# FFN gate and up as seven block products with half of the output product between them

## The chip, the cores and the metric

One core of one Trainium2 chip runs the whole layer in one launch. The metric is the device time of that core in microseconds (us). Before the change three runs gave 1007.88, 1008.01 and 1008.09 us, a median of 1008.01 us.

The engines are called PE (matmul; PEld is its weight load), DVE (vector), ACT (scalar, activations and copies), POOL (GpSimd) and SP (the queue that issues most of the DMAs).

## The reference, cut to what matters

One layer: RMSNorm, a combined input projection, three token mixers, their merge, an output projection with a residual, then the feed-forward network (FFN) with a residual, then a final RMSNorm. The change touches the FFN only. There are 512 rows of 1024 channels; the hidden width is 2816, so 22 tiles of 128.

```python
h2 = rmsnorm(x, ffn_norm_g)
gate, up = jnp.split(h2 @ w_ffn_in, 2, axis=-1)      # (512, 1024) @ (1024, 2 * 2816)
return x + (jax.nn.silu(gate) * up) @ w_ffn_out      # (512, 2816) @ (2816, 1024)
```

## The kernel before

All numbers are float32. The kernel multiplies with three matmuls instead of one: each operand is split into a high part (a copy in fp32r, made by ACT) and a low part (the operand less its high part, made by DVE), and `mm3` (line 164) adds high x high, high x low and low x high into the same PSUM tile.

`h2` holds the normed activations transposed, channels on the partitions: eight tiles k of 128 channels by 512 rows, in two buffers of four k for the high parts and two for the low parts (class `HT`). `norm_B` (line 228) fills them, 128 rows at a time, from PSUM tiles into which PE has transposed the rows: for each half of the channels one copy on ACT and one subtraction on DVE.

The FFN runs over the 22 hidden tiles m (line 1130). For each m the weights of gate and of up (128 x 1024 each) are loaded by SP, split by ACT and DVE (`load_w`, line 159, and `parts`, line 149), and multiplied with h2: two PSUM tiles `ff`, 48 matmuls of 512 columns. ACT takes silu of the gate, DVE multiplies by up, ACT and DVE split the result into a high and a low part. These 22 pairs stay in SBUF, in `hid`, spread over buffers of several pools, because they are needed twice: after each odd m, `ffn_out` multiplies the last two of them with the left 512 output columns of the output weights, into four PSUM tiles `acc` that live through the loop (one for each 128 rows); after the loop all 22 are multiplied with the right 512 columns (`acc2`), in 18 steps over all rows and then the last four row by row, so that the final norm of the first rows runs beside the matmuls of the later ones. The tile m = 0 is done ahead of the loop, in two halves of 256 rows (`ff0`), so that its first half can start before the last 128 rows are normed.

PSUM has eight banks: three for `BIG` (pool pb), five for `SM` (pool pq). SBUF tiles come from pools with a fixed count of buffers for each tag: `w` (raw weights, 3), `wh` and `wl` (2 each), `u` (29 of 512 columns), `d` (8 of 1024), `t` (6 of 512), `o` (4 of 1024).

The order of each engine's queue is set by a scheduler at build time, from the order of the code, dependences, free buffers and priorities; at run time each engine works through its queue in that order. What stands in `tc.high_priority` is put ahead of what isn't, as soon as it has its buffers: the weights are prepared so, as far ahead as their buffers allow.

Of the kernel before, what the change touches and what calls it, by code (L numbers as in the profile page):

```python
# [16 lines left out]
P = 128  # L17
# [40 lines left out]
def trunk(ctx, tc, a, out, dbg=None):  # L58
# [105 lines left out]
    def mm3(ps, lh, ll, rh, rl, first, last):  # L164
        T.matmul(ps, lh, rh, start=first, stop=False)  # L165
        T.matmul(ps, lh, rl, start=False, stop=False)  # L166
        T.matmul(ps, ll, rh, start=False, stop=last)  # L167
# [60 lines left out]
    def norm_B(r, t, o):  # L228
        sl = slice(t * P, (t + 1) * P)
        for n, ph in enumerate(r):  # L230
            A.copy(o.h[n][:, :, sl], ph)
            V.tensor_tensor(o.l[n][:, :, sl], ph, o.h[n][:, :, sl].bitcast(F32), op=ALU.subtract)

# [58 lines left out]
    def cs(c):  # L292
        return slice(c * P, (c + 1) * P)
# [798 lines left out]

    def residual(t):
# [8 lines left out]
    ff0 = []  # L1102
    for t in range(NT):
# [3 lines left out]
        if t > 0:  # L1107
            norm_B(residual(t - 1), t - 1, h2)
    norm_B(residual(NT - 1), NT - 1, h2)
# [8 lines left out]

    acc = [SM("acc") for _ in range(NT)]
    fw = {}  # L1120
    hid = []

    def ffn_out(k, t, n, ps, c=slice(0, 512)):
        if (k // 2, n) not in fw:
            src = a["wfo"][2 * (k // 2):2 * (k // 2) + 2, :, 512 * n:512 * n + 512].rearrange("k p c -> p k c")
            fw[k // 2, n] = load_w(src)
        wh, wl = fw[k // 2, n]
# [4 lines left out]
    for m in range(FT):  # L1132
        pr = ff0 if m == 0 else []
        for g in range(2 if m else 0):
            wh, wl = load_w(a["wfi"][2 * m + g])
            ps = BIG("ff")
            for k in range(KT):
                mm3(ps, wh[:, cs(k)], wl[:, cs(k)], h2.hi(k), h2.lo(k), k == 0, k == KT - 1)
            pr.append(ps)
        s = TT("silu")  # L1140
        last = A.activation(s, pr[0], AF.Silu)
        V.tensor_tensor(s, s, pr[1], op=ALU.mult)  # L1142
        if m < 4:
            ho = op.tile([P, 2, S], F32R, tag="o", name=nm("ho"))
            hh, hl = ho[:, 0], ho[:, 1]
        elif m < 8:
            tg = ("toe", "pt", "sc", "kq")[m - 4]
            hh, hl = XT_("hh", tg, F32R), XT_("hl", tg, F32R)
        else:
            hh, hl = (DD if m < 8 + ND else UU)("hh", F32R)  # L1150
        A.copy(hh, s)
        V.tensor_tensor(hl, s, hh.bitcast(F32), op=ALU.subtract)
# [125 lines left out]
```

## Time and profile before

| | |
|---|---|
| median of three runs | 1008.01 us (1007.88 to 1008.09) |
| the profiled execution's own time | 1008.67 us |
| its span, first to last instruction | 1007.0 us |
| PE busy | 987.1 us, 98%, 5388 matmuls |
| DVE busy | 530.6 us, 53% |
| ACT busy | 442.9 us, 44% |
| POOL busy | 141.5 us, 14% |
| mean granted TensorE clock | 0.997 of full speed |
| moved by DMA | 98.31 MB, mean 98 GB/s |

The span is one execution, on the hardware profiler's clock. Busy times are sums over an engine's instructions; matmuls are pipelined and their records overlap, so the distance between the starts of two of them, not the length of a record, is what one costs in a stream. m = 0 of the FFN starts at 636.33 us, the loop with m = 1 at 649.14 us, and the final output leaves at the end of the span.

### The profile page before, as it was taken

The page shows a single profiled execution, that of the slowest core. Times are in us where ns is not written, and L with a number is a line of the kernel's source. Part 1 is how long each engine was busy: PE and PEld are TensorE (multiplying, and loading weights), DVE is VectorE, ACT ScalarE, POOL GpSimd, SP SyncE. Part 2 cuts the span into 40 slices and gives each one's busy share as a digit, 9 for nine tenths or more (in the row PEclk, how much of TensorE's full clock was granted, in tenths as well). Part 3 has the DMA queues.
Part 4 walks back from the last instruction along what each step waited for, and adds up shares of the span by engine and source line. Part 5 has one row for each costly group of instructions (what it writes and reads, how often), then busy time and mean ns, then how long its engine had stood idle before and what let it go on. Part 6 is the DMA issues. An engine that isn't in the chain of part 4 may idle for free.

```text
span 1007.0 us, 13645 instructions
## 1 busy us (share of the span) xinstructions
PE 987.1 (98%) x5388; PEld 810.6 (80%) x5388; DVE 530.6 (53%) x924; ACT 442.9 (44%) x715; POOL 141.5 (14%) x161
## 2 busy tenths in 40 slices
PE   6999999999999999999999999999999999999996
PEld 5788887778887778778888878988888888888885
DVE  6688846657755687665634355532332333323414
ACT  5376345544646476545535453422222222222313
POOL 5116020000223221341112120000000000000201
PEclk9999999999999999999999999999999999999999
DMA  6424261201222222122122224223222222222222
GB/s 217 169 84 126 87 207 63 75 32 55 102 87 82 84 67 81 58 90 84 64 105 84 105 105 168 84 85 104 102 86 105 88 100 105 85 104 99 90 104 84
DMA packets 33008, 98.31 MB, mean 98 GB/s; under 512 B 3504, under 2 KB 3776, under 8 KB 32944
## 3 DMA queue, kind: packets, MB, share of 16 engines
q1 hardware_dynamic: 31120, 91.14, 25.8%
q0 software_dynamic: 1824, 6.31, 2.3%
q8 instruction: 42, 0.69, 0.3%
q14 instruction: 22, 0.18, 0.1%
HBM read 91.65 MB, written 5.78 MB: 97 GB/s over the span
## 4 chain that ended last, share of the span: by engine, by line
PE 94%; DVE 3%; ACT 1%; DMA 1%; issue 1%; SPq 0%; POOL 0%; DVEq 0%; ACTq 0%; POOLq 0%
PE pj L165 10%; PE pj L166 10%; PE pj L167 10%; PE ff L167 8%; PE ff L165 8%; PE ff L166 8%; PE acc L166 4%; PE acc L165 4%; PE acc L167 4%; PE br L165 2%; PE br L167 2%; PE br L166 2%; PE ov L835 1%; PE pv L165 1%; PE pv L167 1%; PE pv L166 1%
## 5 line engine op out<-in xcount | busy, mean ns | idle before, releaser
L153 ACT CAST wh<-w 128x1024 fp32r<-128x1024 f32 x150 | 157.7, 1051 | 403.7 <-PE ff L166 163.9
L157 DVE TENSOR_TENSOR wl<-w,wh 128x1024 fp32r<-128x1024 f32 x148 | 194.0, 1311 | 251.4 <-ACT wh L153 248.6
L165 PE MATMUL pj<-hTh,wh 128*128 128x512 f32 x464 | 184.4, 397 | 1.0 <-DVE cvo L386 1.0
L166 PE MATMUL pj<-hTl,wh 128*128 128x512 f32 x464 | 183.4, 395 | 0.0
L167 PE MATMUL pj<-hTh,wl 128*128 128x512 f32 x464 | 182.7, 394 | 0.0
L165 PE MATMUL ff<-h2h,wh 128*128 128x512 f32 (+1 forms) x368 | 139.9, 380 | 0.0
L167 PE MATMUL ff<-h2h,wl 128*128 128x512 f32 (+1 forms) x368 | 139.8, 380 | 0.0
L166 PE MATMUL ff<-h2l,wh 128*128 128x512 f32 (+1 forms) x368 | 139.8, 380 | 0.0
L165 PEld LDWEIGHTS pj<-hTh,wh 128*128 128x128 f32 x464 | 87.2, 188 | 19.6 <-ACT wh L153 1.4
L167 PEld LDWEIGHTS pj<-hTh,wl 128*128 128x128 f32 x464 | 87.2, 188 | 17.3 <-issue 0.3
L166 PEld LDWEIGHTS pj<-hTl,wh 128*128 128x128 f32 x464 | 87.2, 188 | 16.5 <-issue 0.3
L166 PEld LDWEIGHTS ff<-h2l,wh 128*128 128x128 f32 x368 | 69.2, 188 | 13.2
L167 PEld LDWEIGHTS ff<-h2h,wl 128*128 128x128 f32 x368 | 69.2, 188 | 13.1
L165 PEld LDWEIGHTS ff<-h2h,wh 128*128 128x128 f32 x368 | 69.2, 188 | 13.0
L166 PE MATMUL acc<-wl,hh 128*128 128x512 f32 (+1 forms) x162 | 59.5, 367 | 0.0
L165 PE MATMUL acc<-wh,hh 128*128 128x512 f32 (+1 forms) x162 | 59.2, 366 | 0.0
L1182 POOL TENSOR_TENSOR x<-x,gb 128x512 f32<-128x512 f32 x4 | 6.0, 1539 | 343.6 <-ACT sq L197 343.6
L1142 DVE TENSOR_TENSOR silu<-silu,ff 128x512 f32<-128x512 f32 x22 | 15.1, 688 | 72.2 <-PE ff L167 72.2
L167 PE MATMUL acc<-wh,hh 128*128 128x512 f32 (+1 forms) x126 | 46.1, 366 | 0.0
L165 PE MATMUL br<-oh,wh 128*128 128x512 f32 x96 | 38.2, 398 | 0.0
L1042 POOL TENSOR_TENSOR y<-y,yt 128x512 f32<-128x512 f32 x16 | 22.5, 1406 | 110.6 <-DVE yt L1041 110.6
L167 PE MATMUL br<-oh,wl 128*128 128x512 f32 x96 | 37.7, 393 | 0.0
(320 smaller groups left out, 1590.3 us busy)
## 6 DMA issues: line engine op xcount, KB each, us to landing
w<-in_wb SPq DMA_DIRECT2D x60, 512.0 KB, 3.5
w<-in_wfi SPq DMA_DIRECT2D x44, 512.0 KB, 3.5
w<-in_wfo SPq DMA_DIRECT2D x22, 512.0 KB, 3.5
w<-in_wbr SPq DMA_DIRECT2D x12, 512.0 KB, 3.5
w<-in_wv SPq DMA_DIRECT2D x8, 512.0 KB, 3.4
w<-in_wout SPq DMA_DIRECT2D x8, 512.0 KB, 3.5
x<-in_x SPq DMA_DIRECT2D x4, 512.0 KB, 6.3
toe<-in_toe SPq DMA_DIRECT2D x8, 256.0 KB, 3.0
```

Of the source, the lines that this page charges most:

```text
L153: A.copy(hi, raw)
L157: (eng or V).tensor_tensor(lo, raw, hi.bitcast(F32), op=ALU.subtract)
L165: T.matmul(ps, lh, rh, start=first, stop=False)
L166: T.matmul(ps, lh, rl, start=False, stop=False)
L167: T.matmul(ps, ll, rh, start=False, stop=last)
L835: T.matmul(po[64 * hh:64 * hh + 64, 0:P], av[kt][:, h * 64:(h + 1) * 64], PT[hh][:, cs(kt)], start=kt == 0, stop=kt == qb, tile_position=( ...
L1042: G.tensor_tensor(y[m], y[m], t, op=ALU.add)
L1142: V.tensor_tensor(s, s, pr[1], op=ALU.mult)
L1182: G.tensor_tensor(xt[0], xt[0], gb[:, 0:512], op=ALU.mult)
```

## The change

For each m from 1 to 21 gate and up are computed together as one block product. The weights of the pair are seen as 2 x 2 blocks (gate or up, by first or second half of the 1024 channels), h2 as 2 x 2 blocks (half of the channels, by half of the rows). Seven products of blocks, with sums and differences of blocks as their operands, replace the eight of the direct way. A product is 4 k-tiles x 3 matmuls of 256 columns.

- The four sums of h2's blocks (T1 to T4) are made once, ahead of the loop, from unsplit copies `xf` that `norm_B` now leaves beside the split ones, and are then split; T4 overwrites a quarter of h2. The three sums of the weights' blocks (`s2`, `s3` and `s2` again) are made for each m by DVE and POOL and split by ACT and DVE, in `ffn_weights`, at high priority.
- Seven products go into three PSUM tiles `pa`, `pm`, `pg` (the three BIG banks), which are each used twice or three times in one m; between, ACT and DVE read them and add up gate and up (`c1`, `u2`, `u3`) in 256-column pieces. A later product accumulates on an earlier one in the same bank.
- Between the third and the fourth product stands `out_half(m - 1)`: the left half of the output product for the hidden tile before, with its own output weights loaded by SP and split, one k at a time.
- Each hidden tile is stored to DRAM (`hd`) by a DMA that ACT issues, and split into two buffers for `out_half`. For the right half of the output product each is loaded back (`hr`) and split a second time.

The diff, with the part that only deletes the old loop shortened:

```diff
--- before.py
+++ after.py
@@ -161,10 +161,11 @@
         with tc.high_priority(offset=HP):
             return parts(load_raw(src, n), n)
 
-    def mm3(ps, lh, ll, rh, rl, first, last):
-        T.matmul(ps, lh, rh, start=first, stop=False)
-        T.matmul(ps, lh, rl, start=False, stop=False)
-        T.matmul(ps, ll, rh, start=False, stop=last)
+    def mm3(ps, lh, ll, rh, rl, first, last, goes_on=False):
+
+        T.matmul(ps, lh, rh, start=first, stop=False, skip_group_check=goes_on)
+        T.matmul(ps, lh, rl, start=False, stop=False, skip_group_check=goes_on)
+        T.matmul(ps, ll, rh, start=False, stop=last, skip_group_check=goes_on)
 
     def preload(after):
 
@@ -225,11 +226,12 @@
             r.append(h4(ps))
         return r
 
-    def norm_B(r, t, o):
+    def norm_B(r, t, o, xf):
         sl = slice(t * P, (t + 1) * P)
         for n, ph in enumerate(r):
             A.copy(o.h[n][:, :, sl], ph)
             V.tensor_tensor(o.l[n][:, :, sl], ph, o.h[n][:, :, sl].bitcast(F32), op=ALU.subtract)
+            A.copy(xf[n][t // 2][:, :, (t % 2) * P:(t % 2) * P + P], ph)
 
     class HT:
 
@@ -1090,6 +1092,8 @@
     h2 = HT("h2")
     w0 = [load_w(a["wfi"][g]) for g in range(2)]
 
+    xf = [[op.tile([P, 4, 256], F32, tag="o", name=nm("xf")) for _ in range(2)] for _ in range(2)]
+
     def residual(t):
         xt = [U("x2") for _ in range(2)]
         for n in range(2):
@@ -1099,14 +1103,13 @@
         x2.append(xt)
         return norm_A(xt, rms_factor(xt), halves(gb), BIG if t < 2 else SM)
 
-    ff0 = []
     for t in range(NT):
         for n in range(2):
             for k in range(KB, KT):
                 out_mm(k, t, n, wo[k, n])
         if t > 0:
-            norm_B(residual(t - 1), t - 1, h2)
-    norm_B(residual(NT - 1), NT - 1, h2)
+            norm_B(residual(t - 1), t - 1, h2, xf)
+    norm_B(residual(NT - 1), NT - 1, h2, xf)
     ff0 = [BIG("ff") for _ in range(2)]
     for half in range(2):
         r = slice(256 * half, 256 * half + 256)
@@ -1116,45 +1119,139 @@
     tap("x2", x2[0][0])
 
 
+
+
+    LH, RH = slice(0, 256), slice(256, 512)
     acc = [SM("acc") for _ in range(NT)]
-    fw = {}
-    hid = []
+    hd = dr.tile([FT * P, S], F32, name="hd")
+
+    def split(src, hi, lo):
+        A.copy(hi, src)
+        V.tensor_tensor(lo, src, hi.bitcast(F32), op=ALU.subtract)
+        return hi, lo
+
+    def hidden(m, h):
+
+        A.dma_start(hd[m * P:(m + 1) * P, :], h)
+        return split(h, *DD("hh", F32R))
+
+    def out_half(k, hp_):
+        with tc.high_priority(offset=HP):
+            raw = XT_("wo", "toe")
+            nc.sync.dma_start(raw, a["wfo"][k, :, 0:512])
+            wh, wl = split(raw, XT_("woh", "pt", F32R), XT_("wol", "sc", F32R))
+        for t in range(NT):
+            mm3(acc[t], hp_[0][:, cs(t)], hp_[1][:, cs(t)], wh, wl, k == 0, k == FT - 1)
+
+    s0, h0 = TT("silu"), U("hid")
+    A.activation(s0, ff0[0], AF.Silu)
+    V.tensor_tensor(h0, s0, ff0[1], op=ALU.mult)
+
+    with tc.high_priority(offset=HP):
+        (x11, x12), (x21, x22) = xf
+        V.tensor_tensor(x11, x12, x11, op=ALU.subtract)
+        G.tensor_tensor(x12, x22, x12, op=ALU.subtract)
+        V.tensor_tensor(x22, x22, x11, op=ALU.subtract)
+
+        def tparts(src, s):
+            return split(src, *[dp.tile([P, 4, 256], F32R, tag="d", name=nm(s + c)) for c in "hl"])
+
+        T2 = tparts(x22, "T2")
+        V.tensor_tensor(x21, x21, x22, op=ALU.subtract)
+        T3 = tparts(x12, "T3")
+        T1 = tparts(x11, "T1")
+
+        T4 = split(x21, h2.h[0][:, :, RH], h2.l[0][:, :, RH])
+    hparts = hidden(0, h0)
+    B11, B21, B22 = [(h2.h[j][:, :, r], h2.l[j][:, :, r]) for j, r in ((0, LH), (1, LH), (1, RH))]
+
+    def cols(p, r):
+        return p[0][:, r], p[1][:, r]
+
+    def ffn_weights(m):
+        with tc.high_priority(offset=HP):
+            L_, R_ = slice(0, 512), slice(512, 1024)
+            u = load_raw(a["wfi"][2 * m + 1])
+            if m % 2:
+                g = load_raw(a["wfi"][2 * m])
+                a11, a12 = halves(g)
+            else:
+                a11, a12 = U("a11"), U("a12")
+                for n, d in enumerate((a11, a12)):
+                    nc.sync.dma_start(d, a["wfi"][2 * m, :, 512 * n:512 * n + 512])
+            a21, a22 = halves(u)
+            s3, s2 = U("s3"), U("s2")
+            gp = [wp.tile([P, 1024], F32R, tag=c, name=nm(c), bufs=2) for c in ("wh", "wl")]
+            up_ = [op.tile([P, 1024], F32R, tag="o", name=nm("wu")) for _ in range(2)]
+            if m % 2:
+                split(g, *gp)
+            else:
+                split(a11, *cols(gp, L_))
+            G.tensor_tensor(s3, a11, a21, op=ALU.subtract)
+            V.tensor_tensor(s2, a22, s3, op=ALU.subtract)
+            r = {1: cols(gp, L_), 2: cols(gp, R_), 5: cols(up_, L_), 4: cols(up_, R_)}
+            r[6] = split(s2, *UU("s2p", F32R))
+            r[7] = split(s3, *UU("s3p", F32R))
+            G.tensor_tensor(a21, a21, a22, op=ALU.add)
+            if not m % 2:
+                split(a12, *cols(gp, R_))
+            V.tensor_tensor(s2, a12, s2, op=ALU.subtract)
+            split(u, *up_)
+            r[3] = split(s2, *UU("s4p", F32R))
+        return r
+
+    def ffn_pair(m, hp_):
+        w = ffn_weights(m)
+        pa, pm, pg = [BIG("ff")[:, LH] for _ in range(3)]
+        e1, e2, h = TT("e1"), TT("e2"), U("hid")
+        c1, u2, u3, g1 = e1[:, LH], e1[:, RH], e2[:, LH], e2[:, RH]
+
+        def product(i, ps, b, first):
+            for k in range(4):
+                mm3(ps, w[i][0][:, cs(k)], w[i][1][:, cs(k)], b[0][:, k], b[1][:, k], first and k == 0, k == 3,
+                    not first)
+
+        product(1, pa, B11, True)
+        A.copy(c1, pa)
+        product(6, pm, T2, True)
+        V.tensor_tensor(u2, pm, c1, op=ALU.add)
+        product(7, pg, T3, True)
+        V.tensor_tensor(u3, pg, c1, op=ALU.add)
+        out_half(m - 1, hp_)
+        product(2, pa, B21, False)
+        A.activation(g1, pa, AF.Silu)
+        product(5, pm, T1, False)
+        V.tensor_tensor(u3, pm, u3, op=ALU.add)
+        product(4, pg, T4, False)
+        V.tensor_tensor(u2, pg, u2, op=ALU.add)
+        V.tensor_tensor(h[:, LH], g1, u2, op=ALU.mult)
+        product(3, pm, B22, False)
+        V.tensor_tensor(c1, pm, c1, op=ALU.add)
+        last = A.activation(c1, c1, AF.Silu)
+        V.tensor_tensor(h[:, RH], c1, u3, op=ALU.mult)
+        return last, hidden(m, h)
+
+    for m in range(1, FT):
+        last, hparts = ffn_pair(m, hparts)
+    out_half(FT - 1, hparts)
+
+
+    fw, hid = {}, {}
 
     def ffn_out(k, t, n, ps, c=slice(0, 512)):
-        if (k // 2, n) not in fw:
-            src = a["wfo"][2 * (k // 2):2 * (k // 2) + 2, :, 512 * n:512 * n + 512].rearrange("k p c -> p k c")
-            fw[k // 2, n] = load_w(src)
-        wh, wl = fw[k // 2, n]
+        if k not in hid:
+            if k % 2 == 0:
+                src = a["wfo"][k:k + 2, :, 512 * n:512 * n + 512].rearrange("k p c -> p k c")
+                fw[k // 2] = load_w(src)
+            with tc.high_priority(offset=HP):
+                raw = U("hr")
+                nc.sync.dma_start(raw, hd[k * P:(k + 1) * P, :])
+                hid[k] = split(raw, *DD("hh", F32R))
+        wh, wl = fw[k // 2]
         hh, hl = hid[k]
         r = slice(512 * (k % 2) + c.start, 512 * (k % 2) + c.stop)
         mm3(ps[:, c], hh[:, cs(t)], hl[:, cs(t)], wh[:, r], wl[:, r], k == 0, k == FT - 1)
 
-    for m in range(FT):
...
-            for k in (m - 1, m):
-                for t in range(NT):
-                    ffn_out(k, t, 0, acc[t])
     preload(last)
     gb = bc_row(2)
 ```

## Rows read from the trace of the kernel before

**Rows 1.** The page, part 1: busy us, share of the span, instructions.
```profile
PE 987.1 (98%) x5388; PEld 810.6 (80%) x5388; DVE 530.6 (53%) x924; ACT 442.9 (44%) x715; POOL 141.5 (14%) x161
```

**Rows 2.** The page, part 4: shares of the chain that ended last.
```profile
PE 94%; DVE 3%; ACT 1%; DMA 1%; issue 1%; SPq 0%; POOL 0%; DVEq 0%; ACTq 0%; POOLq 0%
```

**Rows 3.** Windows, FFN loop: length, busy PE, PEld, DVE, ACT, POOL; clock, DMA, GB/s.
```profile
649.40:932.10 282.70, 282.70 (x1249) 234.07 (x1248) 90.78 (x94) 78.51 (x96) 0.00 (x0) 1.00 0.28 99
```

**Rows 4.** Timeline, PE: first and last of one m's 48 (start, length).
```profile
703.57 0.39 PE L165 MATMUL ff<-h2h,wh 128*128 128x512 f32 x1
...
714.23 0.39 PE L167 MATMUL ff<-h2h,wl 128*128 128x512 f32 x1
```

**Rows 5.** Timeline, PE: the 256-column stream of m = 0, 65 matmuls; next m's first.
```profile
641.35 0.28 PE L166 MATMUL ff<-h2l,wh 128*128 128x256 f32 x1
...
649.02 0.28 PE L167 MATMUL ff<-h2h,wl 128*128 128x256 f32 x1
649.14 0.40 PE L165 MATMUL ff<-h2h,wh 128*128 128x512 f32 x1
```

**Rows 6.** Timeline, DVE and ACT after the last product of that m.
```profile
714.72 0.69 DVE L1142 TENSOR_TENSOR silu<-silu,ff 128x512 f32<-128x512 f32 x1 [3.38 <-PE ff L167]
715.51 1.23 DVE L157 TENSOR_TENSOR wl<-w,wh 128x1024 fp32r<-128x1024 f32 x1
716.66 0.68 DVE L1152 TENSOR_TENSOR hl<-silu,hh 128x512 fp32r<-128x512 f32 x1
...
714.42 1.05 ACT L153 CAST wh<-w 128x1024 fp32r<-128x1024 f32 x1 [3.85 <-PE ff L166]
715.44 0.62 ACT L1151 CAST hh<-silu 128x512 fp32r<-128x512 f32 x1
```

**Rows 7.** Timeline, DVE and POOL at the merge's end.
```profile
551.28 0.68 DVE L1063 TENSOR_TENSOR yh<-y,yh 128x512 fp32r<-128x512 f32 x1
551.88 2.31 DVE L157 TENSOR_TENSOR wl<-w,wh 128x1024 fp32r<-128x1024 f32 x1
...
548.73 1.29 POOL L1042 TENSOR_TENSOR y<-y,yt 128x512 f32<-128x512 f32 x1 [12.38 <-DVE yt L1041]
551.45 1.67 POOL L1042 TENSOR_TENSOR y<-y,yt 128x512 f32<-128x512 f32 x1 [1.43 <-DVE yt L1041]
```

**Rows 8.** Timeline, DVE and POOL in the mixers.
```profile
300.78 0.68 DVE L785 TENSOR_TENSOR kl<-pj,k 64x512 fp32r<-64x512 f32 x1
304.64 0.42 DVE L907 TENSOR_TENSOR kq<-kq,lqk 128x256 f32<-128x256 f32 x1
304.98 0.42 DVE L908 TENSOR_TENSOR kq<-kq,lqk 128x256 f32<-128x256 f32 x1
...
299.87 1.46 POOL L904 TENSOR_TENSOR kq<-g 128x256 f32<-128x256 f32 x1 [10.44 <-PE lv L885]
```

**Rows 9.** Groups by line and shape, ACT: busy us, mean ns; idle before.
```profile
L828 ACT COPY PT<-pT 128x256 f32<-128x256 f32 x8 | 2.9, 372 | 1.9 <-PE pT L826 1.9
L197 ACT ACTIVATE sq<-x 128x256 f32<-128x256 f32 x2 | 0.8, 416 | 1.0 <-DVE x L1177 1.0
```

**Rows 10.** The page, part 6 (KB, us to landing); then timeline, SP: one issue.
```profile
w<-in_wfi SPq DMA_DIRECT2D x44, 512.0 KB, 3.5
...
640.71 0.38 SPq L118 DMA_DIRECT2D w<-in_wfo  x1
```

**Rows 11.** Timeline, ACT and DVE in the norm's end; groups, POOL, 1024-wide.
```profile
636.17 1.08 ACT L231 CAST h2h<-nT 128x512 fp32r<-128x512 f32 x2 [0.47 <-PE nT L224]
637.13 0.65 ACT L197 ACTIVATE sq<-x 128x512 f32<-128x512 f32 x1
640.77 1.25 ACT L231 CAST h2h<-nT 128x512 fp32r<-128x512 f32 x2 [2.00 <-PE nT L224]
...
641.39 1.35 DVE L232 TENSOR_TENSOR h2l<-nT,h2h 128x512 fp32r<-128x512 f32 x2 [0.70 <-ACT h2h L231]
...
L157 POOL TENSOR_TENSOR wl<-w,wh 128x1024 fp32r<-128x1024 f32 x2 | 4.8, 2398 | 4.5 <-ACT wh L153 4.5
```

More of the change, by code (lines that the diff above doesn't have):

```diff
@@ L1130, in ffn_out @@
         mm3(ps[:, c], hh[:, cs(t)], hl[:, cs(t)], wh[:, r], wl[:, r], k == 0, k == FT - 1)
-    for m in range(FT):
[L1133 to L1152, printed above, removed]
-        hid.append((hh, hl))
-        if m % 2 == 1:
-            for k in (m - 1, m):
-                for t in range(NT):
-                    ffn_out(k, t, 0, acc[t])
     preload(last)
```

## The prediction, before the changed kernel was run

> **What bounds the kernel now.** I read the busy times first: PE is busy 987.1 of 1007.0 us, DVE 530.6, ACT 442.9, POOL 141.5 [rows 1]. A busy PE alone could be a waiting one, so next the chain that ended last: 94% of it is PE, 3% DVE [rows 2]. Then the stage that the change rewrites, cut out by time: from 649.40 to 932.10 us PE is busy 282.70 of 282.70 us at granted clock 1.00, DVE 90.78 (32%), ACT 78.51 (28%), POOL nothing [rows 3]. So nothing there waits but the helpers; the stage lasts as long as its matmuls, and its only price is the spacing of matmul starts. (A record's own length, 0.39 us, overlaps the next and prices nothing.) That spacing is 10.66 us over 47 steps, 0.2268 us for 512 columns [rows 4]. DVE and ACT have two thirds of their time free, and this is what the change spends.
>
> The profiled execution took 1008.67 us, its span 1007.0, so 1.67 us lie around it; the median of the runs is 1008.01. I make the sum as differences and set it on 1008.0.
>
> **The products.** For each m from 1 to 21 gate and up were 2 x 8 x 3 = 48 matmuls of 512 columns: 48 x 0.2268 = 10.89 us. They become 7 x 4 x 3 = 84 of 256 columns (12.5% fewer columns, 75% more instructions). The trace has such a stream, m = 0, which runs in halves of 256: 7.67 us for 64 steps, 0.1198 us [rows 5], not half of 0.2268 (0.1134). So 84 x 0.1198 = 10.06 us, 0.83 less for each m, and 21 x 0.83 = 17.4 us at most. The point at which nothing is gained is 10.89 / 84 = 0.1296 us a step. The output half, 12 matmuls of 512 for each m, stays: 2.72 us. The period of one m goes from 13.61 to 12.78 us.
>
> The Trainium skill (TensorE: Matmul & The Clock Gate, Back-to-back issue gap) gives an isolated gap of N/2.4 + 2.5 ns, 215.8 and 109.2 ns here, and warns that weight loads shape a real stream. By it each m would save 1.19 us and the whole 24.9. The stream of 256 shows 119.8 ns, so the row decides, and this extra gain gets 2 chances in 100.
>
> **DVE in the loop.** Each m now has: two 1024-wide subtractions (low parts of gate and up), seven of 512 (s2 twice, s2p, s3p, s4p, the output weights' low part, the hidden tile's), and seven of 256 (u2 twice, u3 twice, c1, two multiplications). Back to back, starts lie 1.15 us apart for 1024 [rows 6], 0.60 for 512 [rows 7] and 0.34 for 256 [rows 8]: 2.30 + 4.20 + 2.38 = 8.9 us. Each alone takes 1.23, 0.68 and 0.42: 10.2 us. Even m split gate in two of 512, 0.05 more. POOL gets two 512-wide operations, 1.29 us alone; the 1024 subtraction that met one took 2.31 us instead of 1.23, so each costs DVE up to 1.08 [rows 7]. Sum 11.1 to 12.4 us of 12.78: 87 to 97%. DVE isn't the bound, but no longer idle.
>
> The same rows hold for which operations? `kl`, which reads PSUM and one SBUF tile, took 0.68 us beside a POOL operation begun 0.91 us earlier [rows 8], no more than 512-wide ones with POOL idle. The Trainium skill (SBUF — State Buffer, Who interferes with whom) says that a DVE instruction with at most one SBUF input doesn't contend with GpSimd. The adds that free PSUM here have one SBUF input; by the rule they're only queued behind held ones. If they were held themselves, each tight one below would lose 0.3 us.
>
> **ACT in the loop:** 2 x 1.05 (1024-wide), five copies of 0.62 [rows 6], one of 0.37 from PSUM and two silus of about 0.42 at 256 columns [rows 9], and the store of the hidden tile, now issued from ACT: at 0 to 0.38 us, which the SP record shows for one issue [rows 10]. 6.4 to 6.8 us of 12.78; hidden.
>
> **The new waits in the loop.** The three PSUM banks are written two or three times in one m, so PE now waits for readers. Five of seven products have 4 us or more between reader and next writer. Two don't: product 3 writes pm when u3 has read product 5, with product 4 between; the next m's product 6 writes pm when c1 has read product 3, with product 1 between. Count from the start of the last matmul: record 0.28, hop to DVE 0.10 (714.62 to 714.72 [rows 4, 6]), the add 0.42, a hop back of about 0.06 (DVE to ACT took 0.03, 715.41 to 715.44): 0.86. PE is there after 13 x 0.12 = 1.56. So 0.70 us may go by in DVE's queue. Behind the add in that queue stand the other epilogue operations and the next weights; ahead of it can stand weights of m + 2, which have the higher priority. A 512 subtraction (0.60) is covered; a 1024 one just begun (1.15) costs 0.45; one held by POOL (2.31 - 0.08) costs 1.5. Bounds per m: 0 and 2 x 1.5 = 3.0. Rows 6 show the case: the low part of the hidden tile stood behind a 1024 one. A given add meets a 1024 one in 2 x 1.15 / 12.78 = 18% of phases and loses little (0.45² / 2 / 1.15 = 0.09); a held one in about as many and loses 0.5. That is near 0.1 an add, 0.2 an m: 4.2 us. I take it.
>
> The hidden tile: product 3, c1, silu, multiplication, store issue, copy, subtraction: 0.38 + 0.42 + 0.45 + 0.45 + 0.38 + 0.65 + 0.71 = 3.4 us; the output half's third matmul, the first to read the low part, is 13 matmuls of 0.12 per product times three later, 0.12 + 4.31 + 0.45 = 4.9. Cover 1.5 us; cost 0, at the most 3 x 1.15 - 1.5 = 2.0 an m if all three DVE steps meet a 1024 one.
>
> The weights come a whole m ahead (two buffers of each), and 512 KB land in 3.5 us [rows 10]; SP has the output weights, the split even gates and, later, the reloads in its one queue, with a period to spare: 0. If that cover went, a late weight would cost up to 3.5 us once.
>
> **Before the loop.** norm_B gets two more copies for each t, 0.55 us each on ACT. Those of t = 2 stand ahead of the square at 637.13, those of t = 3 beside the casts at 640.77 [rows 11]. That chain ends with h2l at 642.74 and slips by 1.1 + 0.55 to 644.4. The second half of m = 0 began 48 x 0.1198 = 5.75 us before 649.14, at 643.4: 1.0 us late (bounds 0 and 1.65). Then the sums and differences: x11 1.15, x12 on POOL 2.4 (its 1024-wide operations [rows 11]), x22 1.15, T2's parts 1.05 and 1.23: 7.0 us from 644.4, 651.4; with one weight subtraction between 652.6. Product 6 is there at 644.4 + 5.75 + 1.44 = 651.6. I take 0.5 (0 to 4.6, three further subtractions and a POOL hold ahead). Together 1.5.
>
> **After it.** Between the last product and the last output half lie 3.4 us, with nothing of the loop to fill them; the second half's matmuls can be put there if their reloaded tiles are in. I take 1.0 (0 to 3.4). The second half: each k has 2.72 us of PE and gains 0.62 on ACT and 0.68 on DVE beside half a weight tile (0.53 and 0.61): hidden, 0. DMA gets 22 stores and 22 loads of 256 KB, 11.5 MB, on queues that are busy 0.28 of that stage [rows 3]: 0.
>
> **Sum:** -17.4 + 4.2 + 1.5 + 1.0 = -10.7 us; 1008.0 - 10.7 = 997.3.
>
> **Rivals.** *A, the adds stand behind the weights (slower).* Place: u3 and c1 on DVE, in each m. For it: DVE 87 to 97% full, weights first, POOL holds. Against it: a 512 subtraction, the commonest, is covered. If both meet a fresh 1024 one: 0.9 x 21 = 18.9; 1008.0 - 17.4 + 2.5 + 18.9 = 1012. It turns the gain when the mean stall passes (17.4 - 2.5) / 21 = 0.71 us an m. Chance 0.20.
> *B, the hidden tile comes late.* One held subtraction (2.23) in its chain less the cover 1.5: 0.73 x 21 = 15.3; 1008.4, no change. For it: three DVE and three ACT steps in turn. Against: that they are spread over three products. Chance 0.12.
> *C, nothing is late.* DVE's operations fall between the adds, the ends are filled: 1008.0 - 17.4 + 1 = 991.6. For it: 1.5 us cover and free ACT. Against: two windows of 0.70. Chance 0.13.
> The forecast has 0.53, the wider spacing gain 0.02.
>
> **Range and chances.** The forecast's own range is 993 to 1004. C brings the low end to 991, A the high one to 1012; beyond lie A with POOL holds and the extra spacing gain, 2 in 10 or less. A change under 0.2% (2 us) can't be told from none here. Forecast, C and the extra gain are faster, 0.68, and of A and B 0.04; slower is most of A and a third of B, 0.19; the rest, 0.09, is within.
>
> **What would show it.** Right: starts of 0.120 us through the products; a period of one m near 13.0 us; PE's idle time ahead of product 3 and of product 6, released by DVE's u3 and c1; DVE near 75 to 90% of the loop and some 512 or 1024 subtractions at more than their 0.68 and 1.23; PE idle 1 to 2 us near 650 and 1 us at the loop's end. B would show as idle time ahead of the output half, released by the hidden tile's parts. Wrong: a spacing of 0.13 or more in the products, PE waiting for weights or a DMA, or a period over 13.6 us.

## The result, and the profile after

The changed kernel took 1083.17 us (median of 4 runs, 1080.68 to 1086.01) beside 1008.03 of the kernel before: ratio 1.0747, 95% interval 1.072 to 1.0773. The forecast was 997.3 with a range of 991 to 1012, so sign and size were wrong. The profiled execution took 1083.01 us, its span 1081.2.

The page of the changed kernel, parts 1, 2 (the 40 slices of PE and of its granted clock) and 4, against [rows 1, 2]:

```profile
PE 1004.8 (93%) x6144; PEld 858.5 (79%) x6144; DVE 694.0 (64%) x1205; ACT 511.4 (47%) x875; POOL 207.4 (19%) x204
...
PE   6999999999999999999999996988889888899896
...
PEclk9999999999999999999999998888999889999999
...
PE 86%; DVE 6%; ACT 3%; issue 2%; DMA 2%; POOL 0%; ACTq 0%; SPq 0%; DVEq 0%; POOLq 0%
```

PE is no longer the whole chain (94% before, 86% now), and both its busy share and its clock have fallen in one place, from slice 25 on (648.7 us): the rewritten stage. Its windows (length; busy PE, PEld, DVE, ACT, POOL with counts; clock, DMA share, GB/s), where [rows 3] had PE busy without a gap at clock 1.00:

```profile
649.60:673.30 23.70, 16.33 (x95) 14.70 (x94) 17.29 (x21) 8.38 (x12) 3.18 (x2) 0.78 0.26 89
673.30:1003.40 330.10, 285.06 (x1920) 268.09 (x1920) 220.29 (x332) 121.75 (x211) 57.69 (x39) 0.91 0.29 94
1003.40:1010.75 7.35, 4.46 (x14) 3.50 (x14) 4.29 (x8) 5.41 (x8) 0.00 (x0) 0.77 0.98 341
```

These are the first m, the other twenty, and the last output product. Each m has one add of c1 behind its product 3 (line 1229), so the instructions of that line (duration min/median/max in ns, start of the first and the last) measure the period:

```profile
L1229 DVE TENSOR_TENSOR e<-ff,e x21: 411/419/425, 673.5 to 1003.5; 128x256 f32<-128x256 f32 x21
```

(1003.5 - 673.5) / 20 = 16.50 us for one m; 13.61 before, 12.98 forecast. Against the forecast:

| part of the span | forecast, us | after, us |
|---|---|---|
| to the first add of c1 | 649.1 + 1.5 + 12.8 = 663.4 | 673.5 |
| twenty m's | 20 x 12.98 = 259.6 | 330.0 |
| from the last add of c1 to the end | 1.0 + 2.7 + 69.5 = 73.2 | 77.7 |
| span | 996.2 | 1081.2 |

(69.5 us lie in the trace of before between the end of its 22nd output half, 937.5, and 1007.0.) Of the 85 us missed, 70 lie in the steady m's, 10 in the first and 4.5 at the end.

**One pair of m's.** The stalls come at every second m. Windows of the changed kernel, one pair of 33.6 us:

```profile
864.00:871.90 7.90, 7.90 (x57) 7.35 (x55) 2.91 (x7) 1.01 (x2) 0.00 (x0) 1.00 0.50 170
871.90:877.30 5.40, 0.69 (x5) 0.35 (x3) 4.74 (x5) 3.25 (x6) 4.84 (x4) 0.93 0.15 53
877.30:884.00 6.70, 6.70 (x31) 6.51 (x32) 6.67 (x8) 2.75 (x5) 1.04 (x1) 0.54 0.20 56
884.00:897.60 13.60, 13.37 (x103) 12.76 (x102) 7.78 (x16) 5.02 (x9) 0.00 (x0) 1.00 0.20 68
```

PE stops for some 5 us, and then works at clock 0.54. Its timeline there (start, length, and in brackets the idle time before and its releaser):

```profile
871.76 0.28 PE L168 MATMUL ff<-h2h,s4p 128*128 128x256 f32 x1
874.97 0.38 PE L166 MATMUL ff<-h2h,wh 128*128 128x256 f32 x1 [2.93 <-ACT wh L1129]
875.20 0.28 PE L167 MATMUL ff<-h2l,wh 128*128 128x256 f32 x1
877.25 0.58 PE L168 MATMUL ff<-h2h,wl 128*128 128x256 f32 x1 [1.77 <-DVE wl L1130]
877.63 0.41 PE L166 MATMUL ff<-h2h,wh 128*128 128x256 f32 x1
...
881.90 0.41 PE L168 MATMUL ff<-T2h,s2p 128*128 128x256 f32 x1
```

Product 1 of the even m waits for the high part of its own gate weights, and two matmuls later for the low part: some 5.2 us beyond the normal spacing (874.97 - 871.88 and 877.25 - 875.32, plus one slow step). The 20 steps from 877.63 to 881.90 are 0.2135 us each, not 0.12: 1.9 us lost, 2.7 with the other slow matmuls. 2 x 12.78 + 5.2 + 2.7 = 33.5. The chain of waits through that place (start, length, what):

```profile
872.08 0.44 DVE e L1229
872.54 0.43 ACT e L1230
872.99 0.87 DVE hid L1231
873.88 0.33 ACTq L1135
874.30 1.15 ACT wh L1129 x2
875.45 1.75 DVE wl L1130
```

It runs from the last add of an odd m over the hidden tile (silu, multiplication, store) into the weights of the *next* m, which should have been ready long before, and on to PE at 877.25. The other engines in that place:

```profile
868.47 0.33 SPq L1141 DMA_DIRECT2D wo<-in_wfo  x1
868.85 0.90 SPq L1181 DMA_DIRECT2D a<-in_wfi  x2
...
872.30 1.26 POOL L1190 TENSOR_TENSOR s<-a,w 128x512 f32<-128x512 f32 x1 [27.96 <-DMA a<-in_wfi]
...
872.99 0.86 DVE L1231 TENSOR_TENSOR hid<-e,e 128x256 f32<-128x256 f32 x1 [0.48 <-ACT e L1230]
873.77 1.75 DVE L1191 TENSOR_TENSOR s<-w,s 128x512 f32<-128x512 f32 x1
875.44 3.44 DVE L1130 TENSOR_TENSOR wl<-a,wh 128x512 fp32r<-128x512 f32 x2
```

SP issues the gate halves of the even m only at 868.85, behind an output weight; POOL had stood 27.96 us for them; and DVE begins with s2 directly behind the hidden tile's last multiplication. With POOL now at work beside them, two low parts take 3.44 us and s2 1.75, where a 512-wide one alone takes 0.68 [rows 7]. The waits of the twenty m's (us in total, times, longest):

```profile
POOL s L1190 <- DMA a<-in_wfi: 161.3, 6, 28.2
POOL s L1190 <- DVE hid L1227: 80.8, 3, 27.5
...
PE ff L166 <- ACT wh L1129: 25.8, 10, 2.9
...
PE ff L168 <- DVE wl L1130: 16.6, 10, 1.9
```

The second row is the odd one: POOL's s3, a sum of weights, is put down to line 1227, the first write of the *hidden tile* of the m ahead. Nothing in the arithmetic ties these two together. What they share is the tag of their buffers: `hid`, `a11`, `a12`, `s3`, `s2` and the split sums all come from `U(...)`. That gave theory A: buffers of one tag are given out in the order of the code, so the tiles of m + 1, which stand behind `h` of m in the code, can't be begun before `h` is, near the end of m.

The row that gave the theory can't carry it, though. At m = 2 the same s3 runs ahead of that write:

```profile
671.98 1.29 POOL L1190 TENSOR_TENSOR s<-a,w 128x512 f32<-128x512 f32 x1 [20.48 <-PE ff L168]
...
672.30 1.24 DVE L1227 TENSOR_TENSOR hid<-e,e 128x256 f32<-128x256 f32 x1
```

And in the three m's of the row s3 starts 2.91 to 2.97 us after the issue of the gate halves, in the other seven even m's 2.77 to 5.95 after it, so the landing of the halves explains all ten; their issue too (868.85 above) comes ahead of the first write (871.17). What the trace does show is a place in a queue: in all ten even m's DVE's s2 stands directly behind the hidden tile's last multiplication (line 1231), as at 873.77. So theory A has to be read as the order in which the queues were built, not as a wait of one tile for another at run time. The rivals were B, the SP queue (the halves behind the output weight); C, later H, POOL's detour; later D, a want of raw-weight buffers, and S, the two ends.

### The profile page after: what moved, and what is told of

It is laid out like the page before. It is cut to its first block, busy times and chain, and to the rows that moved or that the text cites. A ratio compares the mean times of both kernels' runs of the same rounds, so it can differ in the third digit from the quotient of the medians.

```text
span 1081.2 us, 15921 instructions
## 1 busy us (share of the span) xinstructions
PE 1004.8 (93%) x6144; PEld 858.5 (79%) x6144; DVE 694.0 (64%) x1205; ACT 511.4 (47%) x875; POOL 207.4 (19%) x204
## 2 busy tenths in 40 slices
PE   6999999999999999999999996988889888899896
## 4 chain that ended last, share of the span: by engine, by line
PE 86%; DVE 6%; ACT 3%; issue 2%; DMA 2%; POOL 0%; ACTq 0%; SPq 0%; DVEq 0%; POOLq 0%
PE pj L166 10%; PE pj L167 10%; PE pj L168 10%; PE ff L168 7%; PE ff L166 7%; PE ff L167 7%; PE acc L166 3%; PE acc L167 3%; PE acc L168 3%; PE br L166 2%; PE br L168 2%; PE br L167 2%; DVE wl L1130 2%; PE ov L837 1%; PE pv L168 1%
## 5 line engine op out<-in xcount | busy, mean ns | idle before, releaser
L157 DVE TENSOR_TENSOR wl<-w,wh 128x1024 fp32r<-128x1024 f32 x95 | 128.6, 1354 | 112.9 <-ACT wh L153 112.4
L153 ACT CAST wh<-w 128x1024 fp32r<-128x1024 f32 x97 | 101.8, 1049 | 180.7 <-PE pj L167 126.3
L166 PE MATMUL pj<-hTh,wh 128*128 128x512 f32 x464 | 184.4, 397 | 1.0 <-ACT wh L153 1.0
L167 PE MATMUL pj<-hTl,wh 128*128 128x512 f32 x464 | 183.5, 395 | 0.0
L168 PE MATMUL pj<-hTh,wl 128*128 128x512 f32 x464 | 182.7, 394 | 0.0
L166 PEld LDWEIGHTS pj<-hTh,wh 128*128 128x128 f32 x464 | 87.2, 188 | 19.6 <-ACT wh L153 1.4
L168 PEld LDWEIGHTS pj<-hTh,wl 128*128 128x128 f32 x464 | 87.2, 188 | 17.2 <-issue 0.3
L167 PEld LDWEIGHTS pj<-hTl,wh 128*128 128x128 f32 x464 | 87.2, 188 | 16.6 <-issue 0.3
L166 PE MATMUL ff<-h2h,wh 128*128 128x256 f32 x200 | 62.6, 314 | 28.1 <-ACT wh L1129 25.8
L168 PE MATMUL ff<-h2h,wl 128*128 128x256 f32 x200 | 63.6, 318 | 19.6 <-DVE wl L1130 19.6
L166 PEld LDWEIGHTS ff<-h2h,wh 128*128 128x128 f32 x200 | 42.3, 212 | 33.0 <-ACT wh L1129 27.9
L1190 POOL TENSOR_TENSOR s<-a,w 128x512 f32<-128x512 f32 x10 | 12.8, 1282 | 262.6 <-DMA a<-in_wfi 161.3
L167 PE MATMUL ff<-h2l,wh 128*128 128x256 f32 x200 | 60.7, 304 | 0.2 <-DVE h2l L233 0.2
L168 PEld LDWEIGHTS ff<-h2h,wl 128*128 128x128 f32 x200 | 43.3, 216 | 21.9 <-DVE wl L1130 21.9
L1129 ACT CAST woh<-wo 128x512 fp32r<-128x512 f32 x22 | 13.7, 624 | 93.0 <-issue 48.0
L1130 DVE TENSOR_TENSOR wol<-wo,woh 128x512 fp32r<-128x512 f32 x22 | 15.2, 693 | 50.9 <-ACT woh L1129 50.9
L167 PEld LDWEIGHTS ff<-h2l,wh 128*128 128x128 f32 x200 | 42.5, 212 | 1.2 <-DVE h2l L233 0.4
L166 PE MATMUL acc<-woh,hh 128*128 128x512 f32 x88 | 36.5, 415 | 2.9 <-ACT hh L1129 2.9
L166 PE MATMUL acc<-wh,hh 128*128 128x512 f32 (+1 forms) x110 | 38.3, 349 | 0.6 <-DVE x L1260 0.6
L167 PE MATMUL acc<-wl,hh 128*128 128x512 f32 (+1 forms) x110 | 38.5, 350 | 0.0
## 6 DMA issues: line engine op xcount, KB each, us to landing
w<-in_wb SPq DMA_DIRECT2D x60, 512.0 KB, 3.6
w<-in_wfi SPq DMA_DIRECT2D x34, 512.0 KB, 4.1
w<-in_wbr SPq DMA_DIRECT2D x12, 512.0 KB, 3.6
w<-in_wfo SPq DMA_DIRECT2D x11, 512.0 KB, 3.6
```

The lines of the kernel that those rows point to most:

```text
L153: A.copy(hi, raw)
L157: (eng or V).tensor_tensor(lo, raw, hi.bitcast(F32), op=ALU.subtract)
L166: T.matmul(ps, lh, rh, start=first, stop=False, skip_group_check=goes_on)
L167: T.matmul(ps, lh, rl, start=False, stop=False, skip_group_check=goes_on)
L168: T.matmul(ps, ll, rh, start=False, stop=last, skip_group_check=goes_on)
L1129: A.copy(hi, src)
```

## The experiments

The column "one m" is the last start less the first of the add of c1, over 20, from the line's row of each run, as above.

| run | us | ratio to before, 95% | first add | one m |
|---|---|---|---|---|
| changed kernel | 1083.2 | 1.072 to 1.0773 | 673.5 | 16.50 |
| e1 hidden tile's own tag | 1037.4 | 1.0251 to 1.0316 | 684.0 | 13.79 |
| e2 output weight by POOL's queue | 1063.6 | 1.0527 to 1.0569 | 672.8 | 15.51 |
| e3 no POOL | 1061.3 | 1.0503 to 1.0545 | 670.4 | 15.62 |
| e4 = e1 + epilogue first | 1040.0 | 1.0297 to 1.0337 | 674.8 | 14.21 |
| e5 = e1 + four raw buffers | 1040.6 | 1.0308 to 1.0338 | 684.6 | 13.91 |
| e6 = e1 + both | 1039.4 | 1.0298 to 1.0329 | 670.9 | 14.49 |
| e7 = e6 + no POOL | 1014.0 | 1.0041 to 1.0076 | 675.0 | 12.98 |
| e8 = e1 + no POOL | 1028.8 | 1.0182 to 1.0218 | 683.6 | 13.34 |
| e10 = e8 + start and end | 1018.6 | 1.0081 to 1.0111 | 682.6 | 13.14 |
| e11 = e10 + epilogue first | 1009.3 | 0.9995 to 1.0014 | 670.0 | 13.29 |
| e12 = e11 + four raw buffers | 1005.1 | 0.9947 to 0.9977 | 669.2 | 13.02 |
| e13 = changed kernel, 30 buffers | 1084.1 | 1.0738 to 1.077 | 672.0 | 16.62 |
| e14 = changed kernel, weights one m earlier | 1062.5 | 1.0523 to 1.0555 | 684.3 | 14.96 |
| e15 = e12 with POOL again | 1034.1 | 1.0237 to 1.0289 | 669.7 | 14.45 |
| e16 = e12 with the shared tag again | 1055.3 | 1.0449 to 1.0484 | 669.3 | 15.34 |

**One edit at a time on the changed kernel.**

e1, a tag of its own (also for h0):

```diff
-        e1, e2, h = TT("e1"), TT("e2"), U("hid")
+        e1, e2, h = TT("e1"), TT("e2"), XT_("hid", "kq")
```

> The SwiGLU tile leaves the pool tag that it shares with the blocks and sums of the weights; nothing else changes. Theory A (buffers of one tag are handed out in the order of the code, so the weights of m + 1 are ordered behind the first write of the tile of m): the weights are prepared well ahead, the stall ahead of every even m (5.3 us, with 2.7 us of half clock behind it) goes, a pair of m takes 26 to 27 us instead of 33.6, the whole 1005 to 1018 us with what is lost before and after the loop. Rival B (the even gate's load stands in SP's queue behind the output weights' load): that load still stands there, above 1060 us. Rival C (POOL holds DVE in the burst, DVE is too full): the same work on DVE and POOL, above 1045 us.

1037.4: 45.8 us gained by one name. The stall ahead of the even m is gone: PE has no wait for gate weights left in the twenty m's. But the time is 19 to 32 us above what A expected. What is left in its twenty m's:

```profile
DVE s L1191 <- POOL s L1190: 35.7, 16, 5.4
...
PE ff L166 <- DVE e L1224: 15.4, 14, 4.1
```

DVE now stands at s2 waiting for POOL's s3, and the add of u3 (line 1224) that product 3 needs is queued behind it.

e2, the output weight on another queue:

```diff
-            nc.sync.dma_start(raw, a["wfo"][k, :, 0:512])
+            G.dma_start(raw, a["wfo"][k, :, 0:512])
```

> The changed kernel, with the left output weights' load issued by POOL instead of SP; nothing else changes. Rival B: the even gate's halves land 4 to 6 us earlier and the stall goes, 1010 to 1030 us. Theory A: the preparation is ordered behind the tile of the m before on DVE and ACT whenever its data land, so at most 1 to 2 us a pair are won: above 1060 us. Rival C: no change, above 1075 us.

1063.6. The halves are now issued at 848.70, 10.2 us ahead of the hidden tile's last multiplication (858.87) where it was 4.1, and POOL's s3 is done by 856.4; yet s2 starts only at 859.22, directly behind that multiplication, and PE waits as long as before for the high part. So B is not the cause. What the 20 us came from is the wait for the low part: 16.6 us before, 1.3 now that POOL has finished when DVE makes it.

e3, both of POOL's operations of each m on DVE (s3, and the sum of up's two halves, a fourth sum beside the three named under the change):

```diff
-            G.tensor_tensor(s3, a11, a21, op=ALU.subtract)
+            V.tensor_tensor(s3, a11, a21, op=ALU.subtract)
...
-            G.tensor_tensor(a21, a21, a22, op=ALU.add)
+            V.tensor_tensor(a21, a21, a22, op=ALU.add)
```

> The changed kernel, with the two POOL operations of each m (s3 and the sum of up's halves) on DVE; nothing else changes. Rival C (DVE held by POOL in the burst): the held subtractions return to 0.68 and 1.23 us, the burst ahead of even m shortens by 3 us and with it the half clock: 1030 to 1050 us. Theory A: the burst still begins only when the m before is finished; 1055 to 1080 us. Rival B: no change, above 1075 us.

1061.3, as A said: the wait for the high part stays. C's share is again the wait for the low part, which falls from 16.6 to 2.4 us.

e13, the rival to A that the tag was merely short of a buffer:

```diff
-NU, ND, NTMP = 29, 8, 6
+NU, ND, NTMP = 30, 8, 5
```

> The changed kernel with the hidden tile back in the tag of the weights' tiles, but with one buffer more in that tag (30 instead of 29; the ring of temporaries has five instead of six). Theory A (the tiles of the next m wait for the hidden tile because buffers of one tag are given out in the order of the code, not because there are too few of them): no gain, 1075 to 1090. Rival (the tag is one buffer short): about the run with a tag of its own, 1030 to 1045.

1084.1: no gain; one buffer more isn't it. (e1's own tag brings two. Counted from the code, not measured: with 8 tiles of `x2`, 6 split sums of m in use, 10 tiles of an even m + 1 and two hidden tiles, 26 of the 29 are taken at most while one m is prepared ahead.) PE's wait for the high part, 25.8 us in the changed kernel, in e2, e3 and e13:

```profile
PE ff L166 <- ACT wh L1129: 26.8, 10, 3.6
...
PE ff L166 <- ACT wh L1129: 25.5, 10, 3.0
...
PE ff L166 <- ACT wh L1129: 26.6, 10, 3.4
```

Neither SP's order nor POOL nor one buffer more moves it; e1's edit removes it.

e14, the same tag and buffers, another order in the code:

```diff
+    ws = {1: ffn_weights(1)}
...
-        w = ffn_weights(m)
+        w = ws.pop(m)
+        if m + 1 < FT:
+            ws[m + 1] = ffn_weights(m + 1)
```

> The changed kernel with one edit: in the code the preparation of m + 1 comes ahead of the products of m, so that the tiles of m + 2 stand behind the hidden tile of m and no longer right behind that of m + 1; tags and buffers as in the changed kernel. Theory A: the weights of an even m are begun a whole m earlier, and the time falls as with a tag of its own, 1030 to 1050. Rival (the tag of its own helped by its two extra buffers or by another order on DVE): 1070 to 1090.

1062.5: another order, with tags and buffers as they were, brings 20.7 us, so order matters. The proof is weaker than e1's, since the edit also moves the tiles of other tags and what the scheduler ranks first. The number was missed, and the wait moved rather than went. PE's waits in its twenty m's:

```profile
PE acc L166 <- ACT hh L1129: 15.6, 8, 2.1
PE acc L168 <- DVE hh L1130: 9.7, 8, 2.2
```

PE doesn't wait for gate weights any more but for the hidden tile ahead of the output product: the preparation of an even m, now two ahead, still starts directly behind the hidden tile's last multiplication, and the hidden tile's own low part is queued behind it.

**What is left after e1.** Each of the next four runs keeps e1's edit. The edits in short:

```diff
# epilogue first (e4, e6, e7, e11, e12, e15, e16): each add, silu,
# multiplication and split of the hidden tile, h0's too, as here
+        with tc.high_priority(offset=2 * HP):
             V.tensor_tensor(u3, pm, u3, op=ALU.add)
# four raw buffers (e5, e6, e7, e12, e15, e16)
-NU, ND, NTMP = 29, 8, 6
+NU, ND, NTMP = 29, 8, 5
-    wp = ctx.enter_context(tc.tile_pool(name="wp", bufs=3))
+    wp = ctx.enter_context(tc.tile_pool(name="wp", bufs=4))
```

> The run with a buffer tag of its own for the hidden tile (1037.4 us) plus a higher scheduling priority for the adds, silus and splits of the hidden tile, so that they are taken ahead of the next m's weight sums. Theory D (what is left of the loss is the DVE queue standing at the next m's s2, which waits for POOL's s3 and that for up's raw weights, plus a backlog of sums in the first m): the order in the loop hardly changes, so only the first m improves, by some 3 to 6 us of its about 10: 1030 to 1036. Rival E (the order on DVE within a steady m is what costs): 1015 to 1025. Rival F (nothing in it matters): 1036 to 1039.

> The run with a tag of its own for the hidden tile (1037.4 us) plus four buffers instead of three for the raw weights of gate and up; a ring of temporaries has five instead of six buffers to make room. Theory D (the raw up weights come late for want of a buffer, POOL's s3 waits for them, DVE's s2 waits for POOL, and the add that frees the accumulator of product 3 is queued behind): the load is issued earlier, the PE waits on the add of u3 (15.4 us in 14 waits) go to under 5, time 1018 to 1029. Rival G (the load is late for another reason, or the add is late by its own chain): waits as before, 1034 to 1041.

> Both of the two edits together on top of the tag of its own. Theory D: the gains add, 1012 to 1025. If the raw weights decide alone: as the run with four buffers. If neither: 1034 to 1040.

> The three edits together, and POOL's two operations of each m given to DVE (two of about 0.7 us each more on DVE per m, no hold of DVE's subtractions by POOL). Rival H (what is left is the detour by POOL: a wait of DVE for POOL and DVE held while POOL runs): 8 to 20 us under the run without this edit. Theory D, with the wait already gone: within 4 us of it either way, since DVE then has about 1.4 us more per m but no held subtractions.

e4: the first add came 9.2 us earlier, more than expected, but each m grew by 0.42 us, and nothing was gained. e5: no gain; D in that form is wrong. e6: again nothing. e7: 25.4 us at once, the period 12.98. So H holds where D expected 4 us, and the first two edits paid nothing while POOL was in the way. e8 then asks what e7 needs.

> The changed kernel with two edits alone: a tag of its own for the hidden tile, and POOL's two operations of each m given to DVE. Theory H (two causes, the order of the buffers and the detour by POOL; each hides the other, since undoing one alone left 1037.4 and 1061.3): the run of all edits came to 1014.0, so 1012 to 1020. Rival D (the fourth raw buffer or the priority of the epilogue was needed for that): 1025 to 1037. If the two causes simply added: 1083.2 - 45.8 - 21.9 = 1015.5.

1028.8, as D said, and H's number is missed: without POOL, the priority and the fourth buffer are worth the 14.8 us between e8 and e7. In e7 PE's stalls were down to the two ends, but for 1.3 us:

```profile
646.03 1.32 PE L225 MATMUL nT<-cst,xn 128*128 128x128 f32 x8 [2.91 <-DVE xn L222]
...
656.33 0.39 PE L166 MATMUL ff<-h2h,wh 128*128 128x256 f32 x1 [0.97 <-ACT wh L1129]
657.43 0.39 PE L166 MATMUL ff<-T2h,s2p 128*128 128x256 f32 x1 [0.60 <-ACT T2h L1129]
659.82 0.58 PE L168 MATMUL ff<-h2h,wl 128*128 128x256 f32 x1 [2.00 <-DVE wl L1130]
...
937.38 0.50 PE L166 MATMUL acc<-woh,hh 128*128 128x512 f32 x1 [2.89 <-ACT hh L1129]
```

DVE had done sums of the first two m's ahead of the last norm and of the first m's gate weights; at the end nothing was ready but the last hidden tile. e10 mends both:

```diff
+    with tc.high_priority(offset=3 * HP):
         norm_B(residual(NT - 1), NT - 1, h2, xf)
...
-    with tc.high_priority(offset=HP):
+    with tc.high_priority(offset=3 * HP):
         (x11, x12), (x21, x22) = xf
...
-        G.tensor_tensor(x12, x22, x12, op=ALU.subtract)
+        V.tensor_tensor(x12, x22, x12, op=ALU.subtract)
...
-                split(g, *gp)
+                with tc.high_priority(offset=(3 if m == 1 else 0) * HP):
+                    split(g, *gp)
...
-        return split(h, *DD("hh", F32R))
+        return split(h, *((TT("hh", F32R), TT("hl", F32R)) if m == FT - 1 else DD("hh", F32R)))
...
-    out_half(FT - 1, hparts)
+    KF, KE = 18, 4
+    pieces = [[(slice(0, 512), BIG("acc2"))]]
+    for k in range(KE):
+        for r, ps in pieces[0]:
+            ffn_out(k, 0, 1, ps, r)
+    out_half(FT - 1, hparts)
```

> The same two edits, and the two ends mended: at the start the last norm, the T sums (all on DVE) and the split of the first m's gate weights come ahead of the preparation of the first m's; at the end the last hidden tile has buffers of another tag, and four products of the second half (k 0 to 3, first row block, 12 matmuls of 0.227 us) stand ahead of the last output product. In the run of all edits the tensor engine stood 2.91 + 0.97 + 0.60 + 2.00 us at the start and 2.89 us at the end, and ran some 8 us of matmuls at the lower clock behind these. Theory S (these stalls and the clock behind them are the rest): 8 to 12 us under the run with the two edits alone, 1002 to 1010. Rival (stalls move on into the first two m's, where DVE has a backlog): 1011 to 1018.

> The run with both ends mended plus the higher priority of the adds, silus and splits of the hidden tile, so that the sums of the third m no longer stand ahead of them in DVE's order of the first m's. Theory S: 999 to 1007, and at most 2 to 4 us under the run without it, all of it before 690 us. Rival (that priority matters in the steady loop): more than 5 us under it, spread over the m's.

> The run with everything, plus four raw-weight buffers (a ring of temporaries with five instead of six makes room). Theory H: nothing is left that waits for raw weights, so within 2 us of the run without it. Rival D: 3 us or more under it.

e10: 10.2 us under e8, the gain that S gave, but not at its 1002 to 1010, since the base had come to 1028.8. And it came otherwise: the end fell from 77.2 to 71.2 us (span less last add), each m by 0.2, while the first add moved by 1.0 only. There its rival was right in place: the stalls moved on into the first m's, and PE waits 4.80 us at 669.42 for m = 0's hidden tile, whose multiplication (668.59) stands in DVE's queue behind sums of the weights. e11 puts it ahead, at 651.8. e11: 9.3 us more, 12.6 of it before the first add: a miss, since S gave that edit 4 at most; it is what the start needed. e12: 4.2 us more, 0.27 in each m: D's side. e12 is the version that beats both kernels: 1005.07 beside 1008.78, ratio 0.9962 (0.9947 to 0.9977). Its line of c1, its twenty m's as one window, and PE's waits there, one fence for each:

```profile
L1242 DVE TENSOR_TENSOR e<-ff,e x21: 414/417/425, 669.2 to 929.5; 128x256 f32<-128x256 f32 x21
```

```profile
669.20:929.50 260.30, 258.49 (x1918) 245.26 (x1917) 210.17 (x371) 122.62 (x212) 0.00 (x0) 1.00 0.43 142
```

```profile
PE acc L168 <- DVE hh L1131: 1.2, 2, 1.0
PE ff L166 <- DVE e L1234: 0.5, 1, 0.5
```

PE is busy 258.5 of 260.3 us at clock 1.00. That is the forecast's 259.6 for these twenty m's within 1 us, though not by the same terms (see below).

**One cause put back into e12**, to price each when the other is gone:

> The run with everything mended (1005.1) with POOL's two operations of each m given back to POOL. Theory H (the detour by POOL has a price of its own: a wait of DVE and held subtractions): 1020 to 1035. Rival (the detour cost only while the other causes stood): 1003 to 1012.

> The run with everything mended (1005.1) with the hidden tile back in the tag of the weights' tiles. Theory A: preparation of an even m begins at the end of the m ahead again, about 3 to 6 us of stall and lower clock in each of ten pairs: 1035 to 1065. Rival (with priority, four raw buffers and no POOL the order of the buffers no longer matters): 1003 to 1015.

e15, POOL again: 1034.1, 29.1 us. Its timeline shows the price in one place (POOL; DVE; PE):

```profile
806.14 1.29 POOL L1195 TENSOR_TENSOR s<-a,w 128x512 f32<-128x512 f32 x1 [11.20 <-DMA a<-in_wfi]
807.52 1.78 POOL L1200 TENSOR_TENSOR w<-w 128x512 f32<-128x512 f32 x1
...
807.47 0.69 DVE L1196 TENSOR_TENSOR s<-w,s 128x512 f32<-128x512 f32 x1 [1.22 <-POOL s L1195]
808.08 0.42 DVE L1224 TENSOR_TENSOR e<-ff,e 128x256 f32<-128x256 f32 x1
808.42 1.43 DVE L1131 TENSOR_TENSOR hh<-hid,hh 128x512 fp32r<-128x512 f32 x1
...
809.90 0.50 PE L168 MATMUL acc<-woh,hh 128*128 128x512 f32 x1 [1.48 <-DVE hh L1131]
```

DVE stands 1.22 us at s2 for POOL's s3; behind s2 is the low part of the hidden tile, which POOL's second operation then holds to 1.43 us; and the output product's third matmul waits 1.48 us for it. That wait comes in 14 of the twenty m's, 18.7 us in all, in the twelve from 751.67 to 912.05 with 1.45 to 1.48 us each. Of the 28.6 us by which the twenty m's are longer, the rest is mainly two early waits for u3 (2.57 and 1.92 us) and the slow matmuls behind them.

e16, the shared tag again: 1055.3, 50.3 us. DVE begins each even m's sums directly behind the hidden tile's last multiplication again, in ten of ten. With the hidden tile's parts now of higher priority, PE waits ahead of the output product of every second m, 24.4 of the 46.5 us by which its twenty m's are longer; the clock there was 0.91 in windows of 20 us (820 to 840, 840 to 860), and PE is busy 275.0 us instead of 258.5:

```profile
PE acc L166 <- ACT hh L1130: 24.4, 10, 2.4
```

Put back singly the two causes cost 50.3 and 29.1 us. Undone singly on the changed kernel they gave 45.8 and 21.9, 67.7 together; both undone (e8) gave 54.3. So they don't hide each other there, they share a part of the loss, and the smaller causes bind next: the priority and the fourth buffer together gave nothing behind e1 (e6) and 14.8 us once POOL was out. POOL's edit was worth 8.6 us behind e1, 21.9 on the changed kernel, 25.4 behind e6 and 29.1 in e12.

## Why the prediction was wrong, step by step

- **The failed step:** "The weights come a whole m ahead (two buffers of each), and 512 KB land in 3.5 us [...]: 0. If that cover went, a late weight would cost up to 3.5 us once." I counted buffers of the weights and never asked in what order a shared tag gives its buffers out. For even m the cover did go, not once but ten times, and at 5.2 us of stall and 2.7 of slow clock in the pair shown: 79 us at that price, where the twenty m's came to 330.0 - 20 x 12.78 = 74.4 over the bare products. e1 and e16 show that the tag does it; e13, e14 and DVE's queue speak for its order and against its count.
- **The products** were right: 0.12 us a step wherever nothing is late, 10.08 us for the 84 of an m in e12 against 10.06.
- **DVE's load** was right: 220.29 / 20 = 11.0 us for one m of the changed kernel, beside 11.1 to 12.4. In e12 it is 210.17 us in 260.3, 81%, with POOL's work on DVE too.
- **The tight adds** (u3, c1): 0.2 us an m forecast. In e8, with the weights still first and POOL out, PE waits 2.7 us for u3 and 0.8 for c1 in twenty m's, 0.18 an m; the forecast had most of its 0.2 from POOL's holds, so that agreement is partly luck. That e12's period is 0.24 above the bare sum is luck too: PE waits there 0.5 us in all for the adds and 1.2 for the hidden tile, and the output half takes 2.86 us instead of 2.72 (804.52 to 807.38). With POOL in the way (e1) the period was 1.01 above the bare sum, and the u3 add the largest of PE's waits: that is rival A's place and price (0.9), by POOL's late s3 ahead in the queue, not by 1024-wide subtractions.
- **The hidden tile:** forecast 0, at most 2.0 an m; 1.45 to 1.48 in twelve m's of e15. Rival B, with its held subtraction, was right in place and half right in price (0.73), but only behind the other cause. I gave POOL's detour the price of a hold; that DVE's in-order queue *waits* for POOL was not in the sum at all.
- **The start:** 1.5 forecast, 11.6 measured (673.5 against 661.9 without the 1.5): stalls, a DVE backlog of weight sums taken first, and clock 0.78. Weights with the higher priority, which the prediction named for the loop, hurt most here. In e12 7.3 of it are left.
- **The end:** 1.0 forecast, 5.5 measured; nothing stood in PE's queue for the time of the last hidden tile. With other buffers for that tile and four products ahead (e10, e12) it is under the forecast: 71.2 and 71.9 against 73.2.
- **The clock** stood nowhere in the sum, though a stall of 5 us made half as much again in slow matmuls.

e12's profiled span, 1001.4, is 5.2 us above the forecast's 996.2; it is 5.8 us late at the first add. Open stay: by what step the scheduler turns the shared tag into this order of the queues, which no run shows; how the 14.8 us between e8 and e7 share out between priority and the fourth buffer in the loop, and what the smaller ring of temporaries does by itself, which was not tried.

## What to carry to other kernels

A buffer's tag is an ordering constraint as much as a count: before taking "loaded a whole step ahead" for granted, look in the code for what takes a buffer of the same tag between two steps, and in the trace at what stands directly ahead of the late work in its engine's queue. The releaser that a row names is inferred: before building on it, look for a case where the order of the two is the other way round, as at m = 2 here. An engine that runs in order makes one waiting instruction delay all behind it, so an early wait on a side engine can cost more than the work it takes over. Where several causes lie on the same path, the price of one depends on which others stand (POOL's was 8.6 to 29.1 us); put each back singly into the mended kernel to price it there.

## What the chip showed that was not expected

- After PE had been busy 0.69 of 5.40 us, the granted clock fell to the 1.2 GHz level for a while (0.54 over 6.7 us, steps of 0.2135 us). The Trainium skill (TensorE: Matmul & The Clock Gate, Wait — 56ns, not 53.3ns?) gives N / 1.2 GHz from start to start for a cold array; worked out from it, an estimate of 213.3 ns for 256 columns. The rows agree. In e15 the clock stayed at 1.00 through the m's with one stall of 1.45 to 1.48 us each (741.9 to 915.3), while after a stall of 1.92 us at 728.68 it was 0.73 over the next 6.3 us.
- POOL held DVE's 512-wide subtractions of two SBUF tiles to 1.43, 1.75 and, two in a row, 3.44 us, but not the add of u2, which reads PSUM: 0.42 us from 808.08 in e15, within POOL's operation from 807.52. The Trainium skill (SBUF — State Buffer, Who interferes with whom) says that a DVE instruction with at most one SBUF input doesn't contend with GpSimd, and these rows agree.
